# Sliding-window copy on one core: seven upper channels staged in place of eight

## The chip, the core and the metric

The kernel runs on one core of a Trainium2 chip. The metric is the device time of one execution in microseconds (us), and less is better. The profiles are of one execution taken by the hardware profiler; their times count from the start of its span. No matrix work is done: TensorE is idle, and the time goes to DMA engines (16 serve the core) and to copies on VectorE (DVE) and ScalarE (ACT). GpSimd (POOL) and SyncE (SP) issue DMAs.

## What is computed

The input is a batch of 16 images of 64 channels and 64 x 64 float32 values. Every 8 x 8 window at stride 4 is copied to the output, 15 x 15 windows for each image:

```
result = zeros((16, 15, 15, 64, 8, 8))
for i in range(15):
    for j in range(15):
        result[:, i, j] = x[:, :, 4*i : 4*i+8, 4*j : 4*j+8]
```

The input is 16.78 MB and the output 58.98 MB. Nothing is calculated, so the work is to read the input once, to cut it into overlapping windows in the on-chip memory (SBUF), and to write the output.

## The kernel before

**The input tile.** `Lt` holds the whole input in SBUF. Each of the 128 partitions holds 32 channels of 16 image rows of one image: partition = 64 x (half of the channels, `ch`) + 32 x (half of the batch, `y`) + 4 x (image in that half) + (quarter of the image rows, `q`). One channel in one partition is 16 x 64 values, 4 KB, and is one contiguous piece of the input. This text calls such a piece a **row**. The upper half, `ch` = 1, is partitions 64 to 127.

**Two ways in.** Channels 0 to 7 of each half are *staged* (lines 121 to 124): eight DMAs (one for each `q` and `ch`) bring them with 16 partitions each into `GG`, the output buffers that are still unused, in partitions 32 to 95. ACT issues those of `ch` = 0, SP those of `ch` = 1. Then 16 copies (lines 132 to 141, two channels and 32 partitions each) move them into `Lt`: every third on ACT, the others on DVE, in an order written out by hand. The other 24 channels go straight into `Lt` by `load` (line 61), each DMA with 8 partitions, those of one `ch`, `y` and `q`. For each `y` and `q`:

- SP loads channels 12 to 31 of `ch` = 0 (20 channels), for the first six of the eight (`y`, `q`);
- GpSimd loads what is left of `ch` = 0: channels 8 to 11 (4 channels) beside an SP load, or channels 8 to 31 where there is none;
- GpSimd loads channels 8 to 31 of `ch` = 1 (24 channels).

So GpSimd issues 16 loads, in pairs of one for `ch` = 0 and one for `ch` = 1. The loads and the stores of GpSimd share eight completion semaphores in turn, so its ninth load waits until its first has landed, and so on. An SP load waits for a staging DMA of the same semaphore. All DMAs of one issuing engine go through one queue: q10 is ACT's, q1 is SP's, q0 is GpSimd's.

**The output.** Twenty-one output tiles in `GG` are filled by copies and written by scattering DMAs that GpSimd issues (line 158). `part` (lines 185 to 195) makes tiles of 16 KB in each partition for one half of the batch; `plain` and `cross` (lines 203 to 231) make tiles of 24 KB. In `cross` some windows reach over two quarters of the image, so VectorE also shifts between partitions (line 150); 16 partitions of each `cross` tile have no window, and their rows are skipped by an index out of bounds: partitions 64 to 127 with `idx_hi`, 0 to 63 with `idx_lo`. Three buffers of 24 KB are used in turn, after the first three tiles of 16 KB. At the end two stores of 64 partitions (line 257), filled by twelve copies each on ACT and DVE, are issued by SP.

The first `part` tile needs all of the batch's first half (`y` = 0): its staged channels, copied, and its loads. The buffers of the early output tiles overlap the staging area, so they are written only after the staged channels have been copied out.

Of the kernel before, what the change touches and what calls it, by code (L numbers as in the profile page):

```python
# [10 lines left out]
def kernel(  # L11
# [7 lines left out]
    nc = tc.nc  # L19
    P = nc.NUM_PARTITIONS  # L20

    B, C, H, W = x.shape
# [8 lines left out]
    CH = 2  # L31
    HQ = P // (B * CH)
    CL = C // CH
    RB = H // HQ
# [5 lines left out]
    NY = B // YB  # L40
# [11 lines left out]
    L = Lt[:, :, 0 : RB * W].rearrange("p c (r w) -> p c r w", r=RB)  # L52
# [4 lines left out]
    SMALL, HWP = 4, 6  # L57

    def load(eng, ch, y, q, c0, c1):
        p0 = ch * HP + y * QP + q  # L60
        eng.dma_start(out=L[p0 : p0 + QP - HQ + 1 : HQ, c0:c1, :, :], in_=x_v[ch, y, q, :, c0:c1, :])  # L61
# [11 lines left out]
    LF = 3 * CFREE // 2  # L73
# [38 lines left out]

    NG = 3
    TC = CFREE // (RB * W)
    FC = 8
    CP = RB * W + PAD
    GG = gpool.tile([P, NG * LF], f32)
    assert CH * FC * CP <= NG * LF
    S = [GG[:, ch * FC * CP : (ch + 1) * FC * CP].rearrange("p (c f) -> p c f", c=FC)[:, :, 0 : RB * W].rearrange("p c (r w) -> p c r w", r=RB) for ch in range(CH)]
    x_b = x.rearrange("b (ch cl) (hq r) w -> ch hq b cl (r w)", ch=CH, hq=HQ)  # L120
    for q in range(HQ):
        for ch in range(CH):
            s = S[ch][QP + q : QP + q + (B - 1) * HQ + 1 : HQ]
            (nc.scalar, nc.sync)[ch].dma_start(out=s, in_=x_b[ch, q, :, 0:FC, :])

    for y in range(NY):
        for q in range(HQ):
            hw = y * HQ + q < HWP
            if hw:
                load(nc.sync, 0, y, q, FC + SMALL, CL)  # L130
            load(nc.gpsimd, 0, y, q, FC, FC + SMALL if hw else CL)
            load(nc.gpsimd, 1, y, q, FC, CL)

    PC = TC // 2
    first = [(0, ch, c) for ch in range(CH) for c in range(0, FC, PC)]
    then = [(1, ch, c) for ch in range(CH) for c in range(0, FC, PC)]
    for n, (y, ch, c) in enumerate(first + then):
        f = slice(QP + y * QP, QP + (y + 1) * QP)
        d = slice(ch * HP + y * QP, ch * HP + (y + 1) * QP)
        copy = nc.vector.tensor_copy if n % 3 else nc.scalar.copy  # L140
        tc.keep_in_program_order(copy(out=L[d, c : c + PC, :, :], in_=S[ch][f, c : c + PC]))  # L141

    o_v = out.rearrange("b i j c r w -> (b i j) (c r w)")
    o_l = out.rearrange("b i j c r w -> (b i j c r w)").rearrange("(n f) -> n f", f=LF)
# [103 lines left out]
    for s in range(2):  # L248
        t = tile_()
        g = halves(t, 3)  # L250
        for n, ch, cols in line(NR - 1):
            for y in range(NY):
                d = slice(QP + y * QP, QP + (y + 1) * QP)
                f = slice(ch * HP + y * QP, ch * HP + (y + 1) * QP)
# [38 lines left out]
```

## Time and profile before

| | |
|---|---|
| device time, median of 3 runs (lowest to highest) | 185.74 us (185.74 to 185.79) |
| device time of the profiled execution | 185.73 us |
| its span in the profile | 184.0 us |
| read from the chip's main memory (HBM) | 16.78 MB |
| written, with the skipped rows counted | 62.91 MB |

The span is 1.73 us shorter than the time of the same execution. Parts of the profile that the argument uses: the busy share of the DMA engines over time; the packets that each DMA queue moved in a stretch of the span, with a count by size (cumulative: what is under 512 B is also under 8 KB); the queue share, which is the time of the packets over that of 16 engines; and stretches with their bytes per second. A packet is booked to the stretch in which it starts, so in stretches of less than a microsecond the shares jump above and below 1.

### The profile page before, as it was taken

What the parts mean: (1) busy time and instruction counts of PE and PEld (TensorE: products, weight loads), DVE (VectorE), ACT (ScalarE), POOL (GpSimd) and SP (SyncE); (2) the same over time, 40 slices, a digit from 0 to 9 for tenths busy, and PEclk for the clock granted to TensorE, in tenths of its full rate; (3) what the DMA queues carried; (4) which work ended last, traced back from release to release, by engine and by line L of the source; (5) the groups of instructions that cost most, each with busy time, mean ns of one, the idle gap of its engine ahead of it and who ended that gap; (6) DMA issues with size and microseconds to landing.
All of it is one profiled execution on the core that took longest, in us unless ns stands there. A gap on an engine that the chain in (4) does not pass through costs nothing.

```text
span 184.0 us, 501 instructions
## 1 busy us (share of the span) xinstructions
DVE 142.8 (78%) x183; ACT 141.6 (77%) x82; POOL 39.5 (21%) x42
## 2 busy tenths in 40 slices
DVE  4002999999999949979999599898798869978700
ACT  0002999999999969989899489889787869978700
POOL 7500763033330420230122202211220220220000
DMA  4999999999999999999999999999999999999993
GB/s 150 400 412 409 411 413 410 399 394 443 422 431 440 433 431 447 413 435 444 419 438 438 433 429 433 444 433 428 428 428 433 428 435 433 428 428 428 428 428 134
DMA packets 9828, 75.80 MB, mean 412 GB/s; under 512 B 3072, under 2 KB 3072, under 8 KB 7168
## 3 DMA queue, kind: packets, MB, share of 16 engines
q0 software_dynamic: 7504, 64.50, 83.2%
q1 hardware_dynamic: 1744, 9.18, 12.2%
q10 hardware_dynamic: 576, 2.10, 3.1%
q14 instruction: 4, 0.03, 0.0%
HBM read 16.78 MB, written 62.91 MB: 433 GB/s over the span
## 4 chain that ended last, share of the span: by engine, by line
DMA 68%; DVE 19%; issue 3%; POOL 2%; ACT 2%; ACTq 0%; DVEq 0%; PEldq 0%
DMA out_dram<-GG,idx_lo 26%; DMA out_dram<-GG,idx 21%; DMA Lt<-in_x_dram 14%; DVE GG L192 8%; DMA out_dram<-GG,idx_hi 8%; DVE GG L150 7%; POOL Lt L61 2%; ACT GG L256 2%; DVE GG L229 2%; DVE GG L212 1%; ACTq L288 0%; DVE GG L256 0%; DVEq L150 0%; POOL pi L77 0%; DVEq L212 0%
## 5 line engine op out<-in xcount | busy, mean ns | idle before, releaser
L225 ACT COPY GG<-Lt 64x2048 f32<-64x2048 f32 x30 | 56.9, 1897 | 9.6 <-DMA out_dram<-GG,idx 4.8
L150 DVE STREAM_SHUFFLE GG<-Lt 64x1024 f32<-64x1024 f32 (+1 forms) x35 | 50.6, 1444 | 0.9
L192 DVE COPY GG<-Lt 32x2048 f32<-32x2048 f32 x30 | 36.6, 1219 | 4.4 <-DMA out_dram<-GG,idx 3.4
L192 ACT COPY GG<-Lt 32x2048 f32<-32x2048 f32 x18 | 34.1, 1896 | 2.8 <-DMA out_dram<-GG,idx 2.4
L212 ACT COPY GG<-Lt 64x2048 f32<-64x2048 f32 x15 | 28.3, 1897 | 0.8 <-DMA out_dram<-GG,idx_lo 0.5
L141 DVE COPY Lt<-GG 32x2048 f32<-32x2048 f32 x10 | 11.9, 1236 | 13.8 <-DMA GG<-in_x_dram 13.7
L229 DVE COPY GG<-Lt 64x1024 f32<-64x1024 f32 x30 | 20.5, 683 | 0.6
L61 POOL DMA_DIRECT2D Lt<-in_x_dram x16 | 13.8, 873 | 17.5 <-DMA Lt<-in_x_dram 16.8
L158 POOL DMA_INDIRECT out_dram<-GG,idx_y x6 | 9.5, 1578 | 30.7 <-DVE GG L192 26.3
L141 ACT ACT_TABLE_LOAD x1 | 1.3, 1283 | 17.1 <-DMA GG<-in_x_dram 17.1
L212 DVE COPY GG<-Lt 64x2048 f32<-64x2048 f32 x10 | 12.1, 1221 | 0.3
L256 ACT COPY GG<-Lt 32x768 f32<-32x768 f32 x12 | 10.0, 830 | 1.8 <-DMA out_dram<-GG,idx_hi 1.2
L158 POOL DMA_INDIRECT out_dram<-GG,idx_lo x5 | 4.8, 963 | 30.1 <-DVE GG L229 30.1
L141 ACT COPY Lt<-GG 32x2048 f32<-32x2048 f32 x6 | 11.2, 1894 | 0.1
L256 DVE COPY GG<-Lt 32x1280 f32<-32x1280 f32 x12 | 9.8, 819 | 1.6 <-DMA out_dram<-GG,idx_hi 0.9
L158 POOL DMA_INDIRECT out_dram<-GG,idx x5 | 6.2, 1246 | 19.8 <-ACT GG L212 16.7
L158 POOL DMA_INDIRECT out_dram<-GG,idx_hi x5 | 4.9, 976 | 26.0 <-DVE GG L229 18.0
L150 DVE LOAD_MASK_SELECT GG<-Lt x35 | 0.3, 8 | 8.2 <-DMA out_dram<-GG,idx 3.7
L80 DVE TENSOR_SCALAR tb<-pi 128x1 int32<-128x1 int32 x1 | 0.2, 155 | 1.0 <-POOL pi L77 1.0
L83 DVE TENSOR_SCALAR tb<-tb 128x1 int32<-128x1 int32 x2 | 0.3, 153 | 0.0
L86 DVE TENSOR_TENSOR th<-tc,tq 128x1 int32<-128x1 int32 x2 | 0.3, 152 | 0.0
L77 POOL IOTA pi<- 128x1 int32 x1 | 0.1, 124 | 0.4 <-PEq L288 0.4
(20 smaller groups left out, 2.9 us busy)
## 6 DMA issues: line engine op xcount, KB each, us to landing
Lt<-in_x_dram POOLq DMA_DIRECT2D x10, 768.0 KB, 17.8
Lt<-in_x_dram SPq DMA_DIRECT2D x6, 640.0 KB
out_dram<-GG SPq DMA_DIRECT2D x2, 1536.0 KB, 10.1
GG<-in_x_dram ACTq DMA_DIRECT2D x4, 512.0 KB, 14.3
GG<-in_x_dram SPq DMA_DIRECT2D x4, 512.0 KB, 14.7
Lt<-in_x_dram POOLq DMA_DIRECT2D x6, 128.0 KB, 17.8
out_dram<-GG,idx_y POOLq DMA_INDIRECT x6, 12.1
out_dram<-GG,idx POOLq DMA_INDIRECT x5, 13.5
```

The lines of the kernel that those rows point to most:

```text
L61: eng.dma_start(out=L[p0 : p0 + QP - HQ + 1 : HQ, c0:c1, :, :], in_=x_v[ch, y, q, :, c0:c1, :])
L80: nc.vector.tensor_scalar(out=d[:, :], in0=pi[:, :], scalar1=shift, scalar2=mask, op0=ALU.logical_shift_right, op1=ALU.bitwise_and)
L83: nc.vector.tensor_scalar(out=d[:, :], in0=a[:, :], scalar1=float(m), scalar2=None, op0=ALU.mult)
L86: nc.vector.tensor_tensor(out=d[:, :], in0=a[:, :], in1=b[:, :], op=op)
L141: tc.keep_in_program_order(copy(out=L[d, c : c + PC, :, :], in_=S[ch][f, c : c + PC]))
L150: nc.vector.stream_shuffle(out=out, in_=in_, mask=mask)
L158: st = nc.gpsimd.indirect_dma_start(out=rows, out_offset=bass.IndirectOffsetOnAxis(ap=ix[:, 0:1], axis=0), in_=g, in_offset=None, element_ ...
L192: (act if n % 3 == 0 else dve)(out=g[d * QP : (d + 1) * QP, ch], in_=L[f : f + QP, :, s * ST : s * ST + WS, cols],)
L212: (copy or (dve if m else shf))(out=g[d, n], in_=L[f, :, half * ST : half * ST + WS, cols])
L225: act(out=g[lo, n], in_=L[f, :, s * ST : s * ST + WS, cols])
L229: dve(out=g[hi, n, :, 0:ST], in_=L[f, :, (s + 1) * ST : RB, cols])
L256: copy(out=g[d, n, c0:c1], in_=L[f, c0:c1, s * ST : s * ST + WS, cols])
```

## The change

`FC`, the number of staged channels, becomes a pair: eight for `ch` = 0 and seven for `ch` = 1. The four staging DMAs of `ch` = 1 on SP carry 16 partitions of 7 rows in place of 8. GpSimd's eight loads of `ch` = 1 begin at channel 7 in place of 8, and carry 25 channels in place of 24. Of the 16 copies, the last of `ch` = 1 in each half of the batch moves one channel in place of two: one on DVE, one on ACT. The rest of the code is the same two lines further down, and the number and order of the instructions is unchanged.

```
-    FC = 8
+    FC = (8, 7)
...
-            (nc.scalar, nc.sync)[ch].dma_start(out=s, in_=x_b[ch, q, :, 0:FC, :])
+            (nc.scalar, nc.sync)[ch].dma_start(out=s, in_=x_b[ch, q, :, 0 : FC[ch], :])
...
-                load(nc.sync, 0, y, q, FC + SMALL, CL)
-            load(nc.gpsimd, 0, y, q, FC, FC + SMALL if hw else CL)
-            load(nc.gpsimd, 1, y, q, FC, CL)
+                load(nc.sync, 0, y, q, FC[0] + SMALL, CL)
+            load(nc.gpsimd, 0, y, q, FC[0], FC[0] + SMALL if hw else CL)
+            load(nc.gpsimd, 1, y, q, FC[1], CL)
...
-    first = [(0, ch, c) for ch in range(CH) for c in range(0, FC, PC)]
-    then = [(1, ch, c) for ch in range(CH) for c in range(0, FC, PC)]
-    for n, (y, ch, c) in enumerate(first + then):
+    moves = [(y, ch, c) for y in range(NY) for ch in range(CH) for c in range(0, FC[ch], PC)]
+    for n, (y, ch, c) in enumerate(moves):
+        e = min(c + PC, FC[ch])
...
-        tc.keep_in_program_order(copy(out=L[d, c : c + PC, :, :], in_=S[ch][f, c : c + PC]))
+        tc.keep_in_program_order(copy(out=L[d, c:e, :, :], in_=S[ch][f, c:e]))
```

More of the change, by code (lines that the diff above doesn't have):

```diff
@@ L114 @@
     TC = CFREE // (RB * W)
-    FC = 8
+    FC = (8, 7)
     CP = RB * W + PAD
     GG = gpool.tile([P, NG * LF], f32)
-    assert CH * FC * CP <= NG * LF
-    S = [GG[:, ch * FC * CP : (ch + 1) * FC * CP].rearrange("p (c f) -> p c f", c=FC)[:, :, 0 : RB * W].rearrange("p c (r w) -> p c r w", r=RB) for ch in range(CH)]
+    assert sum(FC) * CP <= NG * LF
+    S = [GG[:, ch * FC[0] * CP : (ch * FC[0] + FC[ch]) * CP].rearrange("p (c f) -> p c f", c=FC[ch])[:, :, 0 : RB * W].rearrange("p c (r w) -> p c r w", r=RB) for ch in range(CH)]
     x_b = x.rearrange("b (ch cl) (hq r) w -> ch hq b cl (r w)", ch=CH, hq=HQ)
```

## The prediction

> **What bounds the kernel now.** I read the page first: the busy shares, the slices and the DMA queues.
>
> ```profile
> span 184.0 us, 501 instructions
> ...
> DVE 142.8 (78%) x183; ACT 141.6 (77%) x82; POOL 39.5 (21%) x42
> ...
> DMA  4999999999999999999999999999999999999993
> ...
> DMA packets 9828, 75.80 MB, mean 412 GB/s; under 512 B 3072, under 2 KB 3072, under 8 KB 7168
> ...
> q0 software_dynamic: 7504, 64.50, 83.2%
> q1 hardware_dynamic: 1744, 9.18, 12.2%
> q10 hardware_dynamic: 576, 2.10, 3.1%
> ```
>
> No slice but the first and the last falls below nine tenths of DMA, while both copying engines have a fifth of the span to spare. So the next view is that of the stretches: fill, the store stage, and the end.
>
> ```profile
> 2.00:44.00 42.00, 27.40 (x33) 26.58 (x15) 16.31 (x18) 1.00 1.02 399
> 44.00:173.00 129.00, 113.71 (x141) 114.27 (x68) 22.34 (x20) 1.00 1.01 432
> ```
>
> The last two numbers are the DMA share and GB/s. The share is 1 from 2 us on: each engine has a packet all the time. The time is then what the DMA engines have to move. The change leaves the bytes alone, so only one thing can count: **which** engine moves them, because the span ends when the last of the 16 is done. Hence I looked at how the transfers lie on the engines.
>
> ```profile
> Lt<-in_x_dram POOLq DMA_DIRECT2D x10, 768.0 KB, 17.8
> Lt<-in_x_dram SPq DMA_DIRECT2D x6, 640.0 KB
> ...
> GG<-in_x_dram ACTq DMA_DIRECT2D x4, 512.0 KB, 14.3
> GG<-in_x_dram SPq DMA_DIRECT2D x4, 512.0 KB, 14.7
> Lt<-in_x_dram POOLq DMA_DIRECT2D x6, 128.0 KB, 17.8
> ```
>
> These are the DMA issues. The two queue tables that follow are of 22 to 24 us (an SP load and GpSimd's loads in flight) and of 37 to 39.5 us (SP's loads have ended).
>
> ```profile
> q0 software_dynamic: 202, 0.42, 53.7%
> q1 hardware_dynamic: 100, 0.41, 50.3%
> ```
>
> ```profile
> DMA packets 254, 1.04 MB, mean 416 GB/s; under 512 B 0, under 2 KB 0, under 8 KB 254
> ...
> q0 software_dynamic: 254, 1.04, 101.7%
> ```
>
> In the first, SP's queue takes half of 16 engines and GpSimd's the other half: a load of 8 partitions lies on 8 engines. In the second, GpSimd's queue alone fills all 16, so its loads lie on both groups. I call the eight engines of SP's loads **group S**, and the others **group G**. The reading that fits both tables is that GpSimd's loads alternate: the first of each pair (`ch` = 0) on S, the second (`ch` = 1) on G. The eight staging DMAs have 16 partitions and 128 rows each, 8 rows for each of 16 engines, 64 in all. So an S engine carries 64 + 6 x 20 (SP) + 6 x 4 + 2 x 24 (GpSimd, `ch` = 0) = 256 rows of 4 KB, and a G engine 64 + 8 x 24 = 256. They are level in rows.
>
> They aren't level in short packets. The page counts 3072. GpSimd's loads have 10 x 192 + 6 x 32 = 2112 rows; ten `cross` tiles skip 160 rows; 8 + 16 + 21 + 2 DMAs end with a mark on 16 engines and SP's six loads on 8, which is 800. One short packet for each row of a GpSimd load, each skipped row and each mark gives 2112 + 160 + 800 = 3072, the page's count. So a load of 8 partitions from GpSimd sends a short packet to the other group for each row: in the fill S passes 8 x 24 = 192 of them on each engine, G 6 x 4 + 2 x 24 = 72.
>
> Which group is late? These are the packets of 43.75 to 44.15 us, and of 44.15 to 44.85.
>
> ```profile
> DMA packets 42, 0.22 MB, mean 553 GB/s; under 512 B 6, under 2 KB 6, under 8 KB 36
> ```
>
> ```profile
> DMA packets 239, 0.32 MB, mean 452 GB/s; under 512 B 210, under 2 KB 210, under 8 KB 223
> ```
>
> In the first, 42 - 36 = 6 engines begin to store (packets over 8 KB) and 6 short packets stand beside them: one completion mark each. In the second come 210 short packets, and 223 - 210 = 13 rows of 4 KB. These 210 are the last load's shorts, which lie on S (8 x 24 = 192, plus marks). So G begins to store first (six of its eight engines by 44.15), S after its run of shorts, about half a microsecond later. Stores give each engine the same bytes, at a DMA share of 1.01 throughout: the group that begins last should end last. Stretches of the end:
>
> ```profile
> 179.50:180.50 1.00, 0.00 (x0) 0.00 (x0) 0.00 (x0) 1.00 0.92 393
> 180.50:181.20 0.70, 0.00 (x0) 0.00 (x0) 0.00 (x0) 1.00 0.66 281
> 181.20:181.70 0.50, 0.00 (x0) 0.00 (x0) 0.00 (x0) 1.00 0.00 0
> 181.70:182.20 0.50, 0.00 (x0) 0.00 (x0) 0.00 (x0) 1.00 0.12 49
> ```
>
> A store packet is 24,576 bytes. 393 GB/s for 1 us is 16 packets: each engine begins one. 281 x 0.7 is 8 more, 49 x 0.5 is 1. At 432 / 16 = 27 GB/s a packet lasts 0.91 us. So eight engines end at about 181.1 at the latest, seven by 182.1, and one, which begins its last packet after 181.7, at 182.6 or a little later (I take 182.65). **Half of the DMA engines stand idle for the last 0.9 us.** By the paragraph above the late eight are S.
>
> **The change part by part.** Durations are of the execution of 185.73 us, 184.0 of span and 1.73 around it; the median, 185.74, is the same.
>
> *Staging, four DMAs of SP.* Each drops one row in 16 partitions: 64 rows in all, 4 on each engine. The row that prices them is of 20 to 35.5 us, when only loads run:
>
> ```profile
> 20.00:35.50 15.50, 14.98 (x13) 15.33 (x10) 6.67 (x6) 1.00 1.03 411
> ```
>
> 411 / 16 = 25.7 GB/s, so 4096 bytes take 0.159 us: **-0.64 us** on every engine.
>
> *GpSimd's eight loads.* Eight rows more on each G engine: 8 x 0.159 = +1.28, with the line above **+0.64 us on G**. On S they add no row but 8 short packets. Their cost isn't shown alone. Bounds: nothing, if they pass between other packets; and from the dip around 36 us, where the rate falls:
>
> ```profile
> 35.50:36.00 0.50, 0.47 (x2) 0.50 (x1) 0.00 (x0) 1.00 0.99 393
> 36.00:36.50 0.50, 0.50 (x1) 0.50 (x1) 0.00 (x0) 1.00 1.08 313
> 36.50:37.00 0.50, 0.49 (x2) 0.50 (x1) 0.43 (x1) 1.00 1.21 386
> ```
>
> Against 416 that misses 0.5 x (23 + 103 + 30) = 78 KB, which eight engines move in 0.37 us: at most 15 ns for each of 24. I take half: 8 x 7.5 ns = 0.06 us (0 to 0.12). **S: -0.64 + 0.06 = -0.58 us.**
>
> [...]
>
> *Copies.* One DVE and one ACT copy halve.
>
> ```profile
> L141 DVE COPY Lt<-GG 32x2048 f32<-32x2048 f32 x10 | 11.9, 1236 | 13.8 <-DMA GG<-in_x_dram 13.7
> ...
> L141 ACT COPY Lt<-GG 32x2048 f32<-32x2048 f32 x6 | 11.2, 1894 | 0.1
> ```
>
> That is -0.6 us on DVE and -0.9 on ACT at most, from 17 to 30 us. Worth nothing: the copies that follow wait for loads, and DMA is full meanwhile.
>
> *Later loads.* The upper loads of `y` = 0 put four more short packets on S before the first tile can be filled, each taking a turn with an SP row: up to 4 x 0.32 = 1.3 us if every packet waited a full round of two queues, more likely 4 x 0.16 = 0.64. What hides it is that stores stand in line:
>
> ```profile
> 36.57 1.75 POOL L158 DMA_INDIRECT out_dram<-GG,idx_y  x1 [4.38 <-DMA Lt<-in_x_dram]
> 42.70 1.83 POOL L158 DMA_INDIRECT out_dram<-GG,idx_y  x1 [4.37 <-DVE GG L192]
> ...
> 79.82 1.50 POOL L158 DMA_INDIRECT out_dram<-GG,idx  x1 [3.67 <-ACT GG L212]
> ```
>
> ```profile
> DMA to landing us min/median/max: 9.9/12.6/15.4
> ```
>
> The first store is issued by 38.3 and starts to move at 43.75: 5.4 us of cover. The last row is of all GpSimd's stores: the shortest takes 9.9 us from issue to landing. If that is a 24 KB tile (3.15 MB at 432 GB/s, 7.3 us) and 1.5 is the issue, about 1.1 us of cover remain there; if it is a 16 KB tile, 9.9 - 4.9 - 1.8 = 3.2. Past that point the store queue would run dry.
>
> *GpSimd's issues* grow by a 25th of 0.87 us, 0.03 us each, with loads waiting in the queue ahead of them: nothing.
>
> **Sum.** The last S engine: 182.65 - 0.58 = 182.07. The last of the other S engines: 182.1 - 0.58 = 181.5. G: 181.1 + 0.64 = 181.75. The end is still that one engine's, and 185.73 - 0.58 = **185.15 us**, 0.3% faster. If what holds this one engine back falls elsewhere, G ends last: 182.65 - 181.75 = 0.9 us gained, 184.8.
>
> **Rivals.**
> 1. *G is the last group.* The order at the start of the stores rests on packet counts; over 129 us of stores it could turn, or the late eight may be G for a reason I don't see. Then G's four rows come on top of the end: 185.73 + 0.64 = 186.4, slower. For it: the gap grows from about 0.5 us at 44 to 0.9 at 181, so something else than bytes moves the groups against each other. Against it: it would have to move by over 0.9 us the other way. It decides where G's last engine, now at about 181.1, would end after 182.0 before the change.
> 2. *Nothing moves between engines.* If loads of 8 partitions spread over all 16, four rows leave and four come on each: 185.74. The half shares speak against it. [...]
> 3. *Part of it is eaten:* the shorts cost 15 ns, G drifts later like S does, or a store is issued past its 1.1 us of cover: 185.5.
>
> **How the numbers follow.** The forecast, with the single engine's variant, 0.62 (184.8 to 185.35); part eaten 0.11; no shift 0.11; G last 0.13; a dry queue that costs more than the gain 0.03. A measurement of this kernel can tell about 0.2%, 0.37 us, from no change. Faster by more: 0.64; within: 0.20; slower: 0.16. The range, 184.8 to 185.9, holds all but the last two cases.
>
> **What would show it.** In the profile after: the first stores begin on S, so the run of short packets comes ahead of most of the last 4 KB rows near 44 us; the rows of 4 KB end about 0.6 us later than now on G; at the end the 16 engines finish closer together, with no 0.9 us in which only eight begin a packet; the span is 183.4. The forecast is wrong if eight engines still finish late and later than 182.65, if the dips near 36, 40 and 44 us vanish (loads on all engines), or if a stretch between 50 and 170 us falls under a share of 1.

## The result, and the profile after

| | before | after |
|---|---|---|
| median of 7 runs each (lowest to highest) | 185.74 us (185.65 to 185.80) | 185.08 us (185.03 to 185.25) |
| ratio after to before, 95% interval | | 0.9965 (0.9954 to 0.9977) |
| profiled execution, and its span | 185.73, 184.0 us | 185.05, 183.3 us |

The kernel became 0.66 us faster; 0.59 was forecast. First the page of the profile after: the span, the busy engines, the DMA slices, packets by size (cumulative) and two of the queues.

```profile
span 183.3 us, 501 instructions
...
DVE 142.2 (78%) x183; ACT 140.8 (77%) x82; POOL 40.1 (22%) x42
...
DMA  4999999999999999999999999999999999999995
...
DMA packets 9892, 75.80 MB, mean 414 GB/s; under 512 B 3136, under 2 KB 3136, under 8 KB 7232
...
q0 software_dynamic: 7632, 64.76, 83.8%
q1 hardware_dynamic: 1680, 8.91, 11.9%
```

The bytes are the same 75.80 MB, and DMA is as full as before. SP's queue lost 64 packets (1744 to 1680), the 64 staged rows. GpSimd's queue gained 128: the 64 rows, and 64 short packets, since the page's count under 512 B rose from 3072 to 3136. So each row of a GpSimd load of 8 partitions brings one short packet, as the prediction's count had it.

The decisive view is the start of the stores. These are the packets of 43.75 to 44.15 us and of 44.15 to 44.85, the same stretches as in the prediction.

```profile
DMA packets 208, 0.21 MB, mean 534 GB/s; under 512 B 177, under 2 KB 177, under 8 KB 201
```

```profile
DMA packets 42, 0.32 MB, mean 462 GB/s; under 512 B 5, under 2 KB 5, under 8 KB 28
```

Before, 6 stores and 6 short packets fell into the first stretch and the run of 210 short ones into the second. Now the run (177) comes first, with 208 - 201 = 7 stores begun beside it, and the second stretch has 5 short packets beside 28 - 5 = 23 rows of 4 KB: the short ones are past while eight engines still load. The first stretch has 201 - 177 = 24 rows. Eight engines begin about 20 rows of 0.159 us in 0.4 us, so the rows fill the eight engines of G, and the short packets passed on the others, S. Group S now begins to store first, and G last. The order has turned over, as forecast. The last row of 4 KB begins at 44.9 us, where it was 44.5 before (from narrower windows of the same view): G loads 0.4 us longer, where the prediction had about 0.6.

At the end, the same four stretches (their last two numbers are the DMA share and GB/s; a store packet is 24,576 bytes):

```profile
179.50:180.50 1.00, 0.00 (x0) 0.00 (x0) 0.00 (x0) 1.00 1.03 442
180.50:181.20 0.70, 0.00 (x0) 0.00 (x0) 0.00 (x0) 1.00 0.66 281
181.20:181.70 0.50, 0.00 (x0) 0.00 (x0) 0.00 (x0) 1.00 0.01 0
181.70:182.20 0.50, 0.00 (x0) 0.00 (x0) 0.00 (x0) 1.00 0.00 0
```

The straggler that began a packet after 181.7 is gone; the last packet begins before 181.2. How the groups stand to each other shows best in the DMA view from 178 to 184 us, in 40 slices of 0.15 us. Packets are booked where they begin, so each clump is one round of the engines. First the kernel before, then after:

```profile
DMA  9970009990009990009970000300000000000000
```

```profile
DMA  7379997099997099993330000000000000000000
```

Before, three rounds come in which all sixteen engines begin together, then one of eight, then a single packet: the sixteen are in step, but half of them are a whole packet behind. After, the starts of a round are spread over five to seven slices, where it was three: the engines no longer begin in step.

When they end can be counted too. In both traces each of the last 16 short packets (4 bytes, 9 ns) begins within 4 ns of the end of a store packet: each engine closes its last store with one, a completion mark. These are the marks that begin in each half microsecond (the count under 512 B of the DMA view; 16 in all). Seven lower is an experiment further down:

| | 180.6 to 181.1 | 181.1 to 181.6 | 181.6 to 182.1 | 182.1 to 182.6 | 182.6 to 183.1 |
|---|---|---|---|---|---|
| before | 8 | 0 | 7 | 0 | 1 |
| after | 3 | 10 | 3 | 0 | 0 |
| seven lower | 0 | 8 | 1 | 6 | 1 |

Before, they are the eight, seven and one of the prediction. After, the sixteen end in one group. By the times of the single marks in the trace, the last engine ends at 182.68 before and 181.99 after, while the mean of the sixteen is 181.43 and 181.39: the change saves no work, it only evens out the end.

The first stores were also issued 0.76 us earlier. This is GpSimd's row of time after (start, duration, what the issue waited for); before, they began at 36.57 and 42.70:

```profile
35.81 1.74 POOL L160 DMA_INDIRECT out_dram<-GG,idx_y  x1 [3.13 <-DMA Lt<-in_x_dram]
41.93 1.83 POOL L160 DMA_INDIRECT out_dram<-GG,idx_y  x1 [4.37 <-DVE GG L194]
```

That is a second candidate for the gain, about as large as the gain itself. The experiments had to separate the two.

### The profile page after: what moved, and what is told of

Its sections match the earlier page's. It is cut to its first block, busy times and chain, and to the rows that moved or that the text cites. A ratio compares the mean times of both kernels' runs of the same rounds, so it can differ in the third digit from the quotient of the medians.

```text
span 183.3 us, 501 instructions
## 1 busy us (share of the span) xinstructions
DVE 142.2 (78%) x183; ACT 140.8 (77%) x82; POOL 40.1 (22%) x42
## 2 busy tenths in 40 slices
DMA packets 9892, 75.80 MB, mean 414 GB/s; under 512 B 3136, under 2 KB 3136, under 8 KB 7232
## 3 DMA queue, kind: packets, MB, share of 16 engines
q1 hardware_dynamic: 1680, 8.91, 11.9%
## 4 chain that ended last, share of the span: by engine, by line
DMA 75%; DVE 11%; issue 3%; POOL 3%; ACT 2%; ACTq 0%; DVEq 0%; POOLq 0%; PEldq 0%
DMA out_dram<-GG,idx 28%; DMA out_dram<-GG,idx_lo 21%; DMA Lt<-in_x_dram 19%; DVE GG L152 6%; DMA out_dram<-GG,idx_hi 6%; POOL Lt L61 3%; ACT GG L258 2%; DVE GG L231 2%; DVE GG L214 1%; DVE GG L194 1%; ACTq L290 0%; POOL pi L77 0%; DVEq L152 0%; POOLq L160 0%; PEldq L290 0%
## 5 line engine op out<-in xcount | busy, mean ns | idle before, releaser
L143 DVE COPY Lt<-GG 32x2048 f32<-32x2048 f32 (+1 forms) x10 | 11.4, 1183 | 13.5 <-DMA GG<-in_x_dram 13.4
L61 POOL DMA_DIRECT2D Lt<-in_x_dram x16 | 14.3, 906 | 17.4 <-DMA Lt<-in_x_dram 16.9
L143 ACT COPY Lt<-GG 32x2048 f32<-32x2048 f32 (+1 forms) x6 | 10.3, 1752 | 0.1
```

What stands on the lines that cost most here:

```text
L143: tc.keep_in_program_order(copy(out=L[d, c:e, :, :], in_=S[ch][f, c:e]))
```

## The experiments

Theory **balance**: the gain is the four rows moved from each engine of the late group S to the early group G. Rival **copies**: staging less shortens the copies, so the stores begin earlier. Each kernel was timed beside the kernel before on the same chip (185.61 to 185.75 us there), so ratios are compared.

| kernel | staged, lower and upper | rows on S / G | median us | ratio (95% interval) |
|---|---|---|---|---|
| before | 8, 8 | 256 / 256 | | 1 |
| changed | 8, 7 | 252 / 260 | 185.08 | 0.9965 (0.9954 to 0.9977) |
| changed, again | 8, 7 | 252 / 260 | 184.93 | 0.9961 (0.9948 to 0.9974) |
| copies as before | 8, 7 | 252 / 260 | 184.91 | 0.9959 (0.9946 to 0.9973) |
| seven both | 7, 7 | 256 / 256 | 185.50 | 0.9991 (0.9982 to 1.0000) |
| seven lower | 7, 8 | 260 / 252 | 185.98 | 1.0020 (1.0011 to 1.0029) |
| six upper | 8, 6 | 248 / 264 | 185.27 | 0.9978 (0.9969 to 0.9988) |
| five upper | 8, 5 | 244 / 268 | 185.77 | 1.0006 (0.9997 to 1.0015) |
| four moved | 8, 8 | 252 / 260 | 185.34 | 0.9981 (0.9972 to 0.9990) |
| nine, seven | 9, 7 | 248 / 264 | 185.88 | 1.0006 (0.9997 to 1.0015) |
| seven, six | 7, 6 | 252 / 260 | 185.00 | 0.9967 (0.9955 to 0.9979) |
| five, four | 5, 4 | 252 / 260 | 185.15 | 0.9982 (0.9969 to 0.9994) |

The expectation of five upper names 272 rows for G; that was a slip, it is 52 + 8 x 27 = 268, four more than with six, and the time expected there rests on those four.

**Seven both.** Balance back at level, copies shorter still.

```
-    FC = (8, 7)
+    FC = (7, 7)
```

> Seven channels staged in both halves: both groups of DMA engines carry 256 rows of 4 KB again (S 56 + 6 x 21 + 6 x 4 + 2 x 25, G 56 + 8 x 25), but the copies out of the staging area are shorter still than in the changed kernel. Theory balance (rows moved from the late group S to the early group G made the gain): as before, 185.7 to 185.85 us, S passes 8 more short packets. Rival copies (the gain comes from shorter copies and earlier stores): at least the changed kernel's gain, 185.1 us or less.

Measured: 185.50 us, 0.9991. The gain of the change is gone but for a tenth of a per cent, although the copies are shorter than in the changed kernel, and the first store is as early:

```profile
35.91 1.75 POOL L160 DMA_INDIRECT out_dram<-GG,idx_y  x1 [4.38 <-DMA Lt<-in_x_dram]
```

Copies fall here, and so does the earlier store. The time lies a little under the 185.7 to 185.85 us expected. That the kernel isn't slower, though S passes eight more short packets on each engine, also says that no cost of the short packets can be seen.

**Seven lower.** The mirror image.

```
-    FC = (8, 7)
+    FC = (7, 8)
```

> Seven channels staged in the lower half and eight in the upper: the mirror image. S carries 260 rows and G 252, with the same number of staged channels and shorter copies as in the changed kernel. Balance: S, already late, ends 4 x 0.16 = 0.64 us later, 186.3 to 186.5 us. Copies: the same gain as the change, 185.1 us.

Measured: 185.98 us, 1.0020: slower, as only balance expects, by 0.37 us where 0.64 was expected. The same slices of its end:

```profile
DMA  0079900039930039970009900003000000000000
```

The pattern is that of the kernel before, with its end two to three slices (0.3 to 0.45 us) later: the round of eight stands in the 22nd and 23rd slice, where it stood in the 19th to 21st, and the last packet in the 28th, not the 26th.

**Six upper.** The same direction as the change, twice as far.

```
-    FC = (8, 7)
+    FC = (8, 6)
```

> Six channels staged in the upper half: S 248 rows, G 264. Balance: G now ends last, 0.64 us after where G's last engine ends in the changed kernel (181.8 in its span of 183.3, against 182.0 for the last engine of all), so 0.4 us slower than the changed kernel: 185.4 to 185.6 us. Copies: a second gain of the same size, 184.4 us.

Measured: 185.27 us, 0.9978. The gain turns back, so there is an optimum between; copies would have gained again. Its slices have no empty stretch between the rounds:

```profile
DMA  9337399337399377399373000000000000000000
```

The expected 185.4 to 185.6 was somewhat too slow.

**Copies as before.** The changed kernel's transfers with the kernel before's copying time.

```
-        tc.keep_in_program_order(copy(out=L[d, c:e, :, :], in_=S[ch][f, c:e]))
+        for _ in range(c + PC - e + 1):
+            tc.keep_in_program_order(copy(out=L[d, c:e, :, :], in_=S[ch][f, c:e]))
```

> The changed kernel, but the two copies of one channel are done twice, so that the copying engines work as long as before the change; the transfers are those of the changed kernel. Balance: 185.05 to 185.15 us as the changed kernel. Copies: the gain is gone, 185.7 us.

Measured: 184.91 us, 0.9959, the changed kernel's ratio. Its groups of staging copies, where VectorE is back at the 11.9 us of before and ScalarE at 11.4 (11.2 before):

```profile
L144 DVE COPY Lt<-GG 32x2048 f32<-32x2048 f32 (+1 forms) x11 | 11.9, 1124 | 13.3 <-DMA GG<-in_x_dram 13.2
L144 ACT COPY Lt<-GG 32x2048 f32<-32x2048 f32 (+1 forms) x7 | 11.4, 1650 | 0.1
```

The shorter copies are worth nothing. The other half of the rival, the earlier store, isn't undone here, as the first store goes out as early as in the changed kernel:

```profile
35.76 1.74 POOL L161 DMA_INDIRECT out_dram<-GG,idx_y  x1 [3.14 <-DMA Lt<-in_x_dram]
```

It is seven both, with the early store and no gain, that speaks against it, and the next kernel.

**Four moved.** The rows moved without touching the staging: the last GpSimd load of the lower half is cut so that four of its rows go to G.

```
+            last = (y, q) == (NY - 1, HQ - 1)
-            load(nc.gpsimd, 0, y, q, FC, FC + SMALL if hw else CL)
+            load(nc.gpsimd, 0, y, q, FC, FC + SMALL if hw else CL - 8 if last else CL)
             load(nc.gpsimd, 1, y, q, FC, CL)
+            if last:
+                load(nc.gpsimd, 0, y, q, CL - 8, CL - 4)
+                load(nc.gpsimd, 0, y, q, CL - 4, CL)
```

> The kernel before with its staging and copies untouched; only the last GpSimd load of the lower half is cut in three, so that four of its 24 rows in each partition go to group G: S 252 rows, G 260, as in the changed kernel. Balance: the gain of the change, 0.6 to 0.75 us below the kernel before, about 185.0 us. Rival fewer staged rows (it is the shorter staging that counts): no gain, 185.7.

Measured: 185.34 us, 0.9981. Faster, with all eight channels staged: the shift alone gains. Its first store is even issued 1.8 us later than before (36.57), so an earlier store isn't needed for a gain:

```profile
38.34 2.38 POOL L162 DMA_INDIRECT out_dram<-GG,idx_y  x1 [1.32 <-DMA Lt<-in_x_dram]
```

It gains 0.41 us of an expected 0.6 to 0.75. Two loads more are issued, and the later store or the added loads may take the rest; that wasn't separated.

**Nine, seven.** As many staged rows as before, the rows of six upper.

```
-    FC = (8, 7)
+    FC = (9, 7)
```

> Nine channels staged in the lower half, seven in the upper: as many staged rows as before, S 248 rows and G 264, as in the kernel with six in the upper half. Balance: the time of that kernel, 185.2 to 185.5 us. Fewer staged rows: no gain, 185.7 us or more, as a copy is added.

Measured: 185.88 us, 1.0006: a miss. It is half a microsecond slower than six upper at the same rows. Its first store is issued a microsecond later, six upper's row first:

```profile
36.16 1.75 POOL L160 DMA_INDIRECT out_dram<-GG,idx_y  x1 [3.13 <-ACT GG L194]
```

```profile
37.17 1.74 POOL L160 DMA_INDIRECT out_dram<-GG,idx_y  x1 [4.38 <-DVE GG L194]
```

**Six upper, more copies.** To see whether that microsecond is the cause, six upper with four copies done twice.

```
-    ... for c in range(0, FC[ch], PC)]
+    ... for c in [0] + list(range(0, FC[ch], PC))]
```

> The kernel with six upper channels staged, with four of its staging copies done twice (18 copies, as many as with nine and seven; the transfers are those of six). It is to tell why nine and seven was 0.6 us slower at the same rows for each group. Theory cover: with S ahead of G by 1.8 us the stores stand in line too briefly, and the first store, a microsecond later there (37.2 against 36.2 us), costs time: the same here, 185.6 to 185.9 us. Rival transfers: it is the larger staging itself, so the time stays at 185.3 us.

Measured: 189.60 us, 1.0215. Both expectations miss. A doubled copy that stands on the other engine waited for the first, so VectorE and ScalarE waited for each other (ScalarE 6.1 us in two waits, VectorE 1.5 us in its second), and the first store was issued not 1 but 5.5 us later. The row of the issue, and the stretches in which the stores then ran dry:

```profile
41.66 1.75 POOL L160 DMA_INDIRECT out_dram<-GG,idx_y  x1 [9.26 <-DVE GG L194]
```

```profile
44.00:48.00 4.00, 3.92 (x4) 3.95 (x3) 0.21 (x1) 1.00 1.04 441
48.00:52.00 4.00, 3.91 (x5) 3.95 (x3) 1.62 (x1) 1.00 0.77 322
52.00:56.00 4.00, 3.93 (x5) 3.98 (x3) 1.74 (x1) 1.00 0.77 328
56.00:60.00 4.00, 3.94 (x3) 3.95 (x3) 1.17 (x1) 1.00 0.98 414
```

So it doesn't settle the half microsecond of nine and seven, which stays open. The end marks say only where it is lost: the last is 0.44 us later than in six upper (182.62 against 182.18), and the mean of the sixteen is already 0.30 later (182.00 against 181.70), so most of it is lost before the end and not by an uneven end. The run measures something else: against six upper, 5.5 us of delay cost (1.0215 - 0.9978) x 185.6 = 4.4 us. If each microsecond that counts costs a whole one, 1.1 us of the delay was free; that they do wasn't shown. By this figure, the microsecond of nine and seven should have cost nothing.

**Five upper.** Three steps from the start.

```
-    FC = (8, 7)
+    FC = (8, 5)
```

> Five channels staged in the upper half: S 244 rows, G 272. Balance: G ends last by far and each further row costs its price, so 0.64 us over the kernel with six: 185.8 to 186.0 us. Fewer staged rows: faster again than that kernel.

Measured: 185.77 us, 1.0006. The gain is used up; 0.0028 x 185.7 = 0.52 us over six upper, for four rows priced at 0.64.

**Pair swapped.** The kernel before, with the order of GpSimd's two loads of each pair exchanged.

```
-            load(nc.gpsimd, 0, y, q, FC, FC + SMALL if hw else CL)
             load(nc.gpsimd, 1, y, q, FC, CL)
+            load(nc.gpsimd, 0, y, q, FC, FC + SMALL if hw else CL)
```

> The kernel before with the two loads of each GpSimd pair issued in the other order. If loads of 8 partitions alternate between the groups, the upper half's 192 rows now fall on S beside SP's: S 376 rows, G 136. Balance: S ends 120 x 0.16 = 19 us later, 203 to 206 us. Rival spread (every load on all 16 engines): 185.7 us, no change.

Measured: 211.22 us in one run. Merely the order of the two loads in each pair costs 25 us. That fits loads of 8 partitions that lie on one half of the engines each (SP's queue has 50.3% of 16 engines from 22 to 24 us of the kernel before), GpSimd's on the two halves in turn. Stretches of its profile, and the queues from 36 to 40 us:

```profile
6.00:16.00 10.00, 0.00 (x0) 0.00 (x0) 0.38 (x1) 1.00 1.05 307
16.00:20.00 4.00, 0.00 (x0) 0.00 (x0) 0.00 (x0) 1.00 1.04 255
36.00:40.00 4.00, 0.00 (x0) 0.00 (x0) 1.25 (x2) 1.00 0.53 208
40.00:45.00 5.00, 0.00 (x0) 0.00 (x0) 0.00 (x0) 1.00 0.94 283
60.00:70.00 10.00, 7.83 (x7) 6.46 (x4) 3.44 (x3) 1.00 0.97 325
70.00:200.00 130.00, 110.41 (x137) 112.11 (x66) 20.38 (x18) 1.00 1.00 424
```

```profile
q1 hardware_dynamic: 129, 0.50, 30.2%
q0 software_dynamic: 319, 0.34, 23.1%
```

From 36 to 40 us SP's and GpSimd's queues together fill only half of the engines (a share of 0.53), at 208 GB/s, and loads go on until about 70 us. The time is about 6 us above the expected 203 to 206. Where both groups load, the rows take longer: 307 GB/s at a full share in the first row, where it was 413 in the kernel before, treated below. By the durations worked out there, that stretch lost 10 x (1 - 163 / 224) = 2.7 us. The rate is as low for its share from 16 to 20 us and from 40 to 45; how the rest of the 6 us divides wasn't worked out.

**Less staging at the changed kernel's rows.**

```
-    FC = (8, 7)
+    FC = (7, 6)      and, in the other kernel, (5, 4)
```

> Seven channels staged below and six above: the rows of the changed kernel (S 252, G 260) with one channel less staged in each half. Balance alone: the time of the changed kernel, 185.0 to 185.1 us. If less staging has a worth of its own, as seven and seven hinted (0.1% faster at level rows): 184.8 to 184.95 us.

> Five and four channels staged: again S 252 rows and G 260, with three channels less staged in each half than in the changed kernel. Balance alone: 185.0 to 185.1 us. Worth of less staging: 0.15 us for each channel less, 184.6 us, unless the first tile comes too late.

> The changed kernel on the chip of this group, to compare with: 185.0 to 185.1 us, ratio 0.9965 to the kernel before.

Measured: 185.00 us, 0.9967, and 185.15 us, 0.9982, beside 184.93 us, 0.9961, for the changed kernel on that chip. Less staging shows no worth of its own; what seven and seven hinted isn't confirmed by these two. With five and four the runs spread from 184.84 to 186.33 us. No kernel tried beats the changed one beyond its interval.

## Why the prediction was right, point by point

- *DMA is full, and the group that ends last sets the time.* Right. With staging and copies varied, the time follows the rows of the groups: 260 / 252 slower (1.0020), 256 / 256 as before (0.9991), 252 / 260 fastest (0.9959 to 0.9982), 248 / 264 and 244 / 268 rising again (0.9978 and 1.0006). Nine and seven departs from this line by half a microsecond.
- *Loads of 8 partitions lie on 8 engines, and GpSimd's alternate.* Right: swapping the pairs left half of the engines idle (a share of 0.53 from 36 to 40 us). Loads spread over all 16 engines, the prediction's second rival, would have given no change there, and the run disagrees by 25 us.
- *S is late.* Right: seven lower made it slower (1.0020), after the change the run of short packets (177 from 43.75 to 44.15 us) came ahead of the last rows, and the eight late marks are gone.
- *Four rows less: -0.64 us.* The kind of step is right, and the medians of the change differ by 0.66. That it fits so closely is partly luck, since four rows were worth less in the other pairs: 0.41 in four moved, (0.9991 - 0.9965) x 185.7 = 0.48 from seven both to the change, and 0.37 in seven lower. What takes the difference isn't shown.
- *The short packets on S: +0.06 us.* No run shows such a cost. Seven both has eight more of them on each S engine and wasn't slower (0.9991). Without this term the forecast would have been 0.64.
- *Copies are worth nothing, and stores have about 1.1 us of cover.* Copies: right, as copies as before kept the whole gain. Cover: that there is some fits, since the run with a first store 5.5 us late lost only 4.4, but its size stays open; the prediction had 1.1 or 3.2 us, by which tile the shortest store was.
- *G takes the rows at 0.16 us each, and ends at 181.75.* The direction is right, and nothing speaks against the size: after, fifteen engines end between 180.8 and 181.8. Which of them are G's can't be told from the marks. The price on the late side was less than full: 0.52 for 0.64 from six to five, 0.37 for 0.64 in seven lower. In seven lower, the eight engines that end first do so about 0.4 us later than before, though they should be G's, with four rows less each: the two groups are not independent in the store stage. What ties them together wasn't tried.
- *The single last engine.* It ended at 182.68, and the last mark is now at 181.99, where the forecast had 182.07. Whether that is the same engine, and what held it behind its group before, is not shown.

Left open: why nine and seven is half a microsecond slower than six upper, why four moved got two thirds of the gain, and why four rows paid from 0.37 to 0.66 us for a transfer time of 0.64.

## What to carry to other kernels

When DMA is full from end to end, as here (a share of 1.01 to 1.02 from 2 to 173 us in the kernel before), look at which engines end last: the stretches of the last two microseconds tell whether all sixteen stop together or half of them one packet early. A load of 8 partitions lies on half of the engines here (SP's queue had 50.3% of the 16 from 22 to 24 us, and in pair swapped half of them had no work from 36 to 40 us), so the number of rows in it, and even the order in which loads are issued (25 us in pair swapped), shifts work between the halves; four rows moved from the late half to the early one paid 0.41 to 0.66 us here, for a transfer time of 0.64, and eight or twelve paid less than the change did (ratios 0.9978 and 1.0006 beside 0.9965). A shorter copy or an earlier first store beside it paid no more than 0.1% here, with DMA full: ratios of 0.9961 with the shorter copies and 0.9959 without, and 0.9991 at level rows with the first store 0.66 us earlier.

## What the runs showed of the hardware that was not expected

In the pair swapped kernel (one run), 4 KB rows took longer while both groups loaded. From 6 to 16 us the DMA share was 1.05 and the rate 307 GB/s; in the kernel before, in the same stretch:

```profile
6.00:16.00 10.00, 0.00 (x0) 0.00 (x0) 0.92 (x2) 1.00 1.03 413
```

At the share of 16 engines that is 16 x 1.03 x 4096 / 413 = 163 ns for a row before, and 16 x 1.05 x 4096 / 307 = 224 ns swapped. When S worked alone, from 36 to 40 us, it was back at 16 x 0.53 x 4096 / 208 = 167 ns. The same rows from the same input thus cost a third more. What differs from the kernel before is that group S fills partitions of the upper half, and group G part of the lower half's. That this is the cause, and which of the two it is, wasn't tried.
